# The weight sums of a blocked down projection: VectorE adds, or adding DMAs issued by GpSimd

## The chip, the cores and the metric

The kernel runs on one core of one Trainium2 chip. The core's engines, by the profile's names: PE (TensorE, matmuls; PEld is its loading of weights), DVE (VectorE, elementwise), ACT (ScalarE, elementwise with a function), POOL (GpSimd, elementwise and general) and SP (SyncE, which issues most DMAs). They run side by side, each through its own list of instructions in order, and wait for each other by semaphores. The metric is the device time of one execution in microseconds (us); less is better.

## The reference

The reference is a stack of two encoder layers on 512 tokens of width 1024, all in float32. Each layer mixes tokens (windowed and dilated attention, gates, an output projection, a layer norm) and then runs an MLP. What matters here is the MLP and the norm behind it:

```python
mlp = jnp.einsum('bsf,fd->bsd', jnp.square(jax.nn.relu(
    jnp.einsum('bsd,df->bsf', x, w_up[i]))), w_down[i])
...
x = _layer_norm(DEEPNORM_ALPHA * x + mlp + ple, ln2_g[i], ln2_b[i])
```

`w_up` is 1024 x 4096 and `w_down` 4096 x 1024 in each layer.

## The kernel before

**Precision.** Every float32 operand of a matmul is split in two: a high half (a cast to the type that TensorE takes, by ScalarE, line 225) and a low half (the operand less its high half, by VectorE, line 226). `split` does both. A product of matrices takes three matmuls (high by high, high by low, low by high). Weights come from HBM in chunks of 128 x 1024 numbers (512 KB) that SyncE loads (line 240, tiles `wst`), are split into `whi` and `wlo`, and are used two chunks later.

**Up projection.** The 4096 hidden columns go in four quarters (`q` from 0 to 3), each in eight tiles of 128 columns in the order `UP_ORDER`. Each tile takes 24 matmuls (lines 271 to 273). `Down.hidden` (lines 1013 to 1035) evacuates it: ScalarE takes the ReLU (line 1016), GpSimd squares it (line 1024), and ScalarE and VectorE make the high and low halves of the operands of the down projection: `a11`, `ax` and the sums `sm`. The last of them in a quarter (line 1035, `sml`) is kept as `ready`.

**Down projection.** Within a quarter, the product of the hidden part (as a 2 x 2 block matrix, tokens by hidden) with a 1024 x 1024 block of `w_down` (2 x 2 quadrants) is made in seven block products instead of eight, in the manner of Strassen and Winograd. The table `PRODUCTS` lists them: the operand from the hidden side, the operand from the weights' side, the accumulator, and whether it starts afresh. On the weights' side four of the seven operands are sums of quadrants. With the quadrants called b11, b12, b21 and b22 they are

- T1 = b11 + b12 (product 2), T2 = b11 + b12 + b22 (product 3), T4 = b11 + b12 + b22 + b21 (product 6), all three made one after the other in the tile that b11 was loaded into;
- T3 = b12 + b22 (product 5), made in the tile of b12.

Products 0, 1 and 4 use b11, b21 and b22 as they are. Each quadrant of 512 x 512 lies in two tiles of 128 x 1024 (`c` = 0 and 1), so that a quarter has eight raw tiles of 512 KB and eight sums; two layers of four quarters make 64 loads and 64 sums. `Down.load` (line 988) has SyncE load the eight tiles (line 993); `Down.cut` (line 1006) splits a raw tile as it stands into a set of high and low halves; `Down.add` (line 1002) makes the next sum in place. A sum in the tile of b11 may be made only after the cut before it has read the tile, and the next cut needs the sum: cut b11, add, cut T1, add, cut T2, add, cut T4. With `c` = 0 the halves go into `whi` and `wlo` (three of each, shared with the weights of the up projection), with `c` = 1 into `dhi` and `dlo` (four of each).

`Down.product` (line 1037) makes a block product in two halves of 12 matmuls (line 1051), first over the tiles with `c` = 0 and then with `c` = 1 for each half. Each half's accumulator is evacuated by VectorE (`gather`, line 1070; `spread`, line 1061) into the residual tiles `yt` and into `v`.

**Order.** TensorE runs in the order in which the code is written (`manual_schedule`). The other engines' instructions are put in order by the compiler, by dependences and by a simulation of its own; it makes the cuts and sums with `c` = 1 up to a quarter ahead, during the products of the quarter before. In two places the code sets order itself: `behind` puts the cuts and sums that follow a half product on VectorE behind `ready` (`tc.issue_after`, which queues the block's instructions behind the named one on the named one's engine), and behind the last quarter TensorE, VectorE and ScalarE all follow the code. During the seven products T2 with `c` = 0 is made between product 0's calls of `behind` and product 3: the cut of T1 and the sum of T2 are called behind the second half of product 0, the cut of T2 behind the second half of product 1.

GpSimd makes the squares in the up projection and has no work in the products. SyncE issues all loads in order; the next quarter's raw tiles are loaded as soon as the cuts and sums that read the buffers are done. The program sets the scratch for dynamic DMAs to 1024 bytes per partition.

Of the kernel before, what the change touches and what calls it, by code (L numbers as in the profile page):

```python
# [14 lines left out]
ALU = mybir.AluOpType  # L15
# [5 lines left out]
P = 128  # L21
# [179 lines left out]
def build(nc, tc, plan, down, xT, pT, wst, vec, sink, cst, outT):  # L201
# [3 lines left out]
    with ctx:  # L205
# [4 lines left out]
        def bank(tag, name):  # L210
            return pp.tile([P, 512], F32, tag=tag, name=name, bufs={"mm": 3, "s": 2, "pt": 2, "o": 1}[tag])
# [18 lines left out]
        down_at = {key: int(offs[len(plan) + n]) for n, (key, _) in enumerate(down)}  # L230
        ready, fetched = {}, {}
        at = [0, 0, 0]
# [18 lines left out]
        def ahead(last, further=0):  # L251
            while at[1] < len(plan) and at[1] <= max(last, further):
                fetch(at[1])
                at[1] += 1
                if at[1] - 1 <= last:
                    prep(at[2])
                    at[2] += 1
            while at[2] < len(plan) and at[2] <= last:
                prep(at[2])
                at[2] += 1  # L260

        def weights(key, look=LOOK, further=0):
            c = at[0]
            assert plan[c][0] == key, (plan[c][0], key)
            at[0] += 1
            ahead(c + look, c + further)
            return ready.pop(c)

        def mm3(ps, w, i, x, start, stop):
            s = slice(i * P, (i + 1) * P)  # L270
            nc.tensor.matmul(ps, w[0][:, s], x[0], start=start, stop=False)  # L271
            nc.tensor.matmul(ps, w[0][:, s], x[1], start=False, stop=False)  # L272
            nc.tensor.matmul(ps, w[1][:, s], x[0], start=False, stop=stop)  # L273

        def linear(key, xs, ps=None):
            w = weights(key)
            if ps is None:
                ps = bank("mm", "ps_" + "_".join(str(v) for v in key))
            for i, x in enumerate(xs):
                mm3(ps, w, i, x, i == 0, i == len(xs) - 1)  # L280
            return ps
# [527 lines left out]
        class Norm:  # L809
# [3 lines left out]
            def add(self, out, ps, y):  # L813
                if self.alpha == 1.0:
                    nc.vector.tensor_tensor(out, ps, y, ALU.add)
                else:
                    nc.vector.scalar_tensor_tensor(out, y, self.alpha, ps, ALU.mult, ALU.add)
# [79 lines left out]
            def behind(self, ins):  # L897
                tc.add_manual_dep(ins.ins, self.last.ins.name, mybir.DependencyInfo(
                    mybir.DependencyClass.Sync, mybir.DependencyReason.DATA), reason="statistics first")
# [59 lines left out]
        class Down:  # L959
# [28 lines left out]
            def load(self, q):  # L988
                for d, j in ((0, 0), (1, 0), (1, 1), (0, 1)):
                    for c in range(2):  # L990
                        r = self.qp.tile([P, 1024], F32, name=f"raw{self.l}_{q}_{j}{d}{c}", tag=f"raw{j}{d}{c}", bufs=1)
                        o = down_at[self.l, q, j, d, c]
                        nc.sync.dma_start(r, wst[o:o + P * 1024].rearrange("(p n) -> p n", p=P))
                        self.raw[j, d, c] = r

            def chain(self, n, c):

                b11, b12, b21, b22 = (self.raw[j, d, c] for j, d in ((0, 0), (0, 1), (1, 0), (1, 1)))
                return {"B11": (b11, None), "T1": (b11, b12), "T2": (b11, b22), "T4": (b11, b21),
                        "B22": (b22, None), "B21": (b21, None), "T3": (b12, b22)}[self.PRODUCTS[n][1]]  # L1000

            def add(self, n, c):
                to, other = self.chain(n, c)
                nc.vector.tensor_tensor(to, to, other, ALU.add)  # L1004

            def cut(self, q, n, c):
                pool, tag, bufs = (self.qp, "d", 4) if c else (wp, "w", 3)
# [137 lines left out]
        def pool(name, side="left"):  # L1145
            c = ExitStack()
            return c.enter_context(tc.tile_pool(name=name, bufs=1, side=side, reuse_waits="tile")), c.close
# [3 lines left out]
        for l in range(DEPTH):  # L1151
# [96 lines left out]
            dn = Down(l, qp, None)  # L1248

            def residual_turned(a):  # L1250
                for d in range(2):
                    tp = bank(("pt", "s")[a % 2], f"yT{l}_{a}_{d}")
                    for i in range(4):
                        nc.tensor.transpose(tp[:, i * P:(i + 1) * P], y[4 * d + i][:, a * P:(a + 1) * P], ident)
                    nc.scalar.copy(dn.y[a][:, d * 512:(d + 1) * 512], tp)
# [3 lines left out]
            with tc.manual_schedule(engines={PE}):  # L1259
                pss = []  # L1260
                for i in range(2):
                    pss.append(linear((l, ("up", 0, UP_ORDER[i])), X))
                    residual_turned(2 * i)
                    residual_turned(2 * i + 1)
                yp_close()
                p0_close()
                hp, hp_close = pool(f"hp{l}", "right")
                dn.hp = hp
                dn.operands()
                for q in range(FQ):  # L1270
                    for i, m in enumerate(UP_ORDER):
                        if not i:
                            dn.load(q)
                        if q or i > 1:
                            w = weights((l, ("up", q, m)), (2, 2, 2, 2, 2, 1, 1, 0)[i], min(3, 7 - i))
                            ps = bank("mm", f"ps_up{l}_{q}_{m}")
                            for k, x in enumerate(X):
                                mm3(ps, w, k, x, k == 0, k == KT - 1)
                        else:
                            ps = pss[i]  # L1280
                        dn.hidden(q, m, ps)
                        if i == 2:
                            dn.cut(q, 0, 1)
                        if q == FQ - 1 and i in (1, 2):
                            dn.spread(i - 1, dn.v[i - 1])
                        if i == 3:
                            dn.add(2, 1)
                            dn.cut(q, 1, 1)
                        if i == 4:
                            dn.add(5, 1)  # L1290
                        if i == 5:
                            dn.cut(q, 0, 0)
                        if i == 6:
                            dn.add(2, 0)
                            dn.add(5, 0)
                            dn.cut(q, 2, 1)
                        if i == 7:
                            dn.cut(q, 1, 0)
                            dn.add(3, 1)
                            dn.cut(q, 3, 1)  # L1300
                            dn.add(6, 1)
                    def behind(n, s):

                        with tc.issue_after(dn.ready.ins):
                            if n < 4:
                                if s:
                                    dn.cut(q, n + 2, 0)
                                    if n in (0, 1):
                                        dn.add((3, 6)[n], 0)
                                elif n:  # L1310
                                    dn.cut(q, n + 3, 1)
                            elif n == 4:
                                if not s:
                                    dn.cut(q, 6, 0)
                            elif s:
                                ahead(at[0] + n - 5, at[0] + 2)
                        if q == FQ - 1 and n == 1:
                            dn.moments(s, 0)

                    for n in range(7 if q < FQ - 1 else 4):  # L1320
                        dn.product(q, n, lambda s: behind(n, s))
                if not last:
                    ph, pl = (qp.tile([P, 2, S], F32R, name=f"p{e}{l + 1}", tag=f"raw11{i}", bufs=1) for i, e in enumerate("hl"))
                    pf = qp.tile([P, 2, S], F32, name=f"pf{l + 1}", tag="raw100", bufs=1)
                    nc.sync.dma_start(pf, pT[l + 1])
            q = FQ - 1
# [78 lines left out]
```

## Time and profile before

| | |
|---|---|
| median of 3 runs | 1571.31 us (1571.17 to 1573.22) |
| the profiled execution's own time | 1573.54 us |
| its span, first to last instruction | 1571.8 us |
| mean granted TensorE clock | 0.996 of full speed |
| DMA traffic | 143.37 MB, mean 91 GB/s |
| instructions of the sums (line 1004) | 64 on VectorE |
| loads of raw tiles (line 993) | 64 of 512 KB, median 4.4 us from issue to landing |

How to read the profile: a row of a group gives line, engine, operation, what it writes and reads (buffer numbers left out, so that all raw tiles are `raw`), the shape, the count, then busy us and the mean ns of one, then the engine's idle time ahead of it with what ended that ("releaser"). A row in order of time gives the start in us, the duration in us, engine, line, operation, tiles, and in brackets the idle time ahead and its releaser; neighbours of one kind are merged ("x2"). A row of a stretch gives its bounds, its length, and for PE, PEld, DVE, ACT and POOL the busy time with the number of instructions, then the granted clock, the share of the DMA engines and GB/s. A row of a line's answer gives the count, the shortest, median and longest duration in ns, and the first and last start. Rows of waits give us in total and how many times. Matmuls overlap: each shows as 0.39 us though one follows another in less. A DMA's "landing" is counted from its issue.

### The profile page before, as it was taken

How to read it: one execution, taken by the hardware profiler on the slowest of the kernel's cores; microseconds unless marked ns; L12 is line 12 of the kernel's file. 1: busy time of each engine (PE TensorE's matmuls, PEld its weight loads, DVE VectorE, ACT ScalarE, POOL GpSimd, SP SyncE). 2: the span in 40 equal slices, each digit the busy share in tenths (PEclk: the TensorE clock that was granted, in tenths of full speed). 3: DMA queues.
4: the chain of work that ended last, by engine and by line, in shares of the span. 5: the costliest groups of instructions: out<-in, count | busy, mean ns of one | idle time of the engine just before them, and what ended most of it. 6: DMA issues, size and time to landing. Idle time of an engine off the chain costs nothing.

```text
span 1571.8 us, 19688 instructions
## 1 busy us (share of the span) xinstructions
PE 1533.4 (98%) x7482; PEld 1254.0 (80%) x7482; DVE 1079.9 (69%) x1759; ACT 741.6 (47%) x1237; POOL 288.4 (18%) x208
## 2 busy tenths in 40 slices
PE   8999999999999999999899999999999999999997
PEld 6777888878888888888677778888887888888886
DVE  6878674454947777686868786744549476777867
ACT  4666554333644443434445665543336444434343
POOL 1010100157111111202000101101572111112020
PEclk9999999999999999999999999999999999999999
DMA  6212122232532414141132112223325324241401
GB/s 216 68 54 67 55 82 85 90 104 77 221 94 69 132 56 151 49 148 41 40 106 68 54 57 66 78 79 99 95 79 206 103 75 128 65 149 46 142 1 54
DMA packets 42736, 143.37 MB, mean 91 GB/s; under 512 B 5136, under 2 KB 7312, under 8 KB 42640
## 3 DMA queue, kind: packets, MB, share of 16 engines
q1 hardware_dynamic: 42064, 142.03, 28.4%
q8 instruction: 59, 0.97, 0.3%
q14 instruction: 37, 0.30, 0.1%
q10 hardware_dynamic: 576, 0.07, 0.0%
HBM read 139.98 MB, written 2.10 MB: 90 GB/s over the span
## 4 chain that ended last, share of the span: by engine, by line
PE 86%; DVE 8%; ACT 3%; issue 2%; DMA 1%; SPq 0%; ACTq 0%; DVEq 0%
PE dn L1051 16%; PE ps_up L273 7%; PE ps_up L272 7%; PE ps_up L271 7%; DVE wlo L226 2%; PE sa L399 1%; PE pta L377 1%; PE ps_start L271 1%; PE ps_start L272 1%; PE sb L399 1%; PE ps_start L273 1%; PE ya L271 1%; PE ya L273 1%; PE ya L272 1%; PE ps_pg L272 1%
## 5 line engine op out<-in xcount | busy, mean ns | idle before, releaser
L226 DVE TENSOR_TENSOR wlo<-wst,whi 128x1024 fp32r<-128x1024 f32 (+1 forms) x197 | 261.7, 1332 | 184.6 <-ACT whi L225 167.8
L225 ACT CAST whi<-wst 128x1024 fp32r<-128x1024 f32 (+1 forms) x197 | 202.3, 1029 | 352.8 <-PE ps_up L272 106.7
L1024 POOL TENSOR_TENSOR hr<-r 128x512 f32<-128x512 f32 x64 | 102.1, 1595 | 568.5 <-ACT r L1016 568.5
L271 PE MATMUL ps_up<-xhi,whi 128*128 128x512 f32 x480 | 186.9, 389 | 0.0
L273 PE MATMUL ps_up<-xhi,wlo 128*128 128x512 f32 x480 | 186.7, 389 | 0.0
L272 PE MATMUL ps_up<-xlo,whi 128*128 128x512 f32 x480 | 186.7, 389 | 0.0
L225 ACT CAST whi<-raw 128x1024 fp32r<-128x1024 f32 x56 | 58.0, 1052 | 101.4 <-PE ps_up L272 62.0
L272 PEld LDWEIGHTS ps_up<-xlo,whi 128*128 128x128 f32 x480 | 90.1, 188 | 18.8
L271 PEld LDWEIGHTS ps_up<-xhi,whi 128*128 128x128 f32 x480 | 90.1, 188 | 18.7
L273 PEld LDWEIGHTS ps_up<-xhi,wlo 128*128 128x128 f32 x480 | 90.1, 188 | 18.5
L225 ACT CAST dhi<-raw 128x1024 fp32r<-128x1024 f32 x56 | 58.8, 1052 | 82.8 <-PE dn L1051 59.5
L1070 DVE TENSOR_TENSOR yt<-yt,dn 128x512 f32<-128x512 f32 x96 | 65.3, 682 | 43.4 <-PE dn L1051 43.4
L1004 DVE TENSOR_TENSOR raw<-raw,raw 128x1024 f32<-128x1024 f32 x64 | 86.4, 1350 | 0.9 <-DMA raw<-wst 0.7
L226 DVE TENSOR_TENSOR wlo<-raw,whi 128x1024 fp32r<-128x1024 f32 x56 | 68.2, 1221 | 17.8 <-ACT whi L225 17.8
L226 DVE TENSOR_TENSOR dlo<-raw,dhi 128x1024 fp32r<-128x1024 f32 x56 | 68.2, 1220 | 5.1 <-ACT dhi L225 5.1
L336 POOL TENSOR_TENSOR sw_qb<-sw_qb,ct 128x512 f32<-128x512 f32 x12 | 18.4, 1536 | 181.9 <-DVE sw_qb L334 181.9
L1051 PE MATMUL dn<-whi,smh 128*128 128x512 f32 x128 | 50.1, 394 | 0.7 <-DVE yt L1070 0.7
L1051 PE MATMUL dn<-wlo,smh 128*128 128x512 f32 x128 | 50.6, 395 | 0.2
L1211 POOL TENSOR_TENSOR gate<-gate,gate 128x512 f32<-128x512 f32 x16 | 25.0, 1585 | 140.2 <-DVE gate L1210 140.2
L1051 PE MATMUL dn<-whi,sml 128*128 128x512 f32 x128 | 49.9, 390 | 0.0
L1051 PE MATMUL dn<-dhi,smh 128*128 128x512 f32 x128 | 49.9, 389 | 0.0
L1051 PE MATMUL dn<-dlo,smh 128*128 128x512 f32 x128 | 49.8, 389 | 0.0
(1015 smaller groups left out, 4048.0 us busy)
## 6 DMA issues: line engine op xcount, KB each, us to landing
wst<-wst SPq DMA_DIRECT2D x187, 512.0 KB, 3.6
raw<-wst SPq DMA_DIRECT2D x64, 512.0 KB, 4.4
wst<-wst SPq DMA_DIRECT2D x10, 256.0 KB, 2.7
xs<-xT SPq DMA_DIRECT2D x8, 256.0 KB, 4.7
outT<-nt SPq DMA_DIRECT2D x8, 256.0 KB, 2.2
ct<-cst SPq DMA_DIRECT2D x2, 960.0 KB, 8.0
pf<-pT SPq DMA_DIRECT2D x4, 256.0 KB, 4.0
pf<-pT SPq DMA_DIRECT2D x1, 512.0 KB, 3.5
```

Of the source, the lines that this page charges most:

```text
L225: nc.scalar.copy(hi, src)
L226: nc.vector.tensor_tensor(lo, src, hi.bitcast(F32), ALU.subtract)
L271: nc.tensor.matmul(ps, w[0][:, s], x[0], start=start, stop=False)
L272: nc.tensor.matmul(ps, w[0][:, s], x[1], start=False, stop=False)
L273: nc.tensor.matmul(ps, w[1][:, s], x[0], start=False, stop=stop)
L336: nc.gpsimd.tensor_tensor(sw, sw, cc["sin"], ALU.mult)
L399: nc.tensor.matmul(ss[r][:, col], q[a][rs, qs], k[b][rs, ks], start=n == 0, stop=n == 2)
L1004: nc.vector.tensor_tensor(to, to, other, ALU.add)
L1024: nc.gpsimd.tensor_tensor(h.rearrange("p s t -> p (s t)"), r, r, ALU.mult)
L1051: nc.tensor.matmul(ps[s], a[:, k, tok], w[b][:, cols], start=first and not (k or m), stop=k == 3 and m == 2, skip_group_check=True)
L1070: return nc.vector.tensor_tensor(to, to, ps, ALU.subtract if n in (2, 4, 5) else ALU.add)
L1211: nc.gpsimd.tensor_tensor(g, g, ga[t], ALU.add)
```

## The change

The sums are no longer VectorE instructions with both quadrants in SBUF. GpSimd issues a DMA that reads the other quadrant from HBM again and adds it to the tile in place. The calls of `add` get the quarter as an argument and stand where they stood; `at` is the slice of the packed weights from which `load` takes a quadrant too. The call inside `behind` (the sums of T2 and T4 with `c` = 0) is still inside `tc.issue_after(dn.ready.ins)`, which names a VectorE instruction.

```diff
-                        o = down_at[self.l, q, j, d, c]
-                        nc.sync.dma_start(r, wst[o:o + P * 1024].rearrange("(p n) -> p n", p=P))
+                        nc.sync.dma_start(r, self.at(q, j, d, c))
                         self.raw[j, d, c] = r
 
+            def at(self, q, j, d, c):
+                o = down_at[self.l, q, j, d, c]
+                return wst[o:o + P * 1024].rearrange("(p n) -> p n", p=P)
+
             def chain(self, n, c):
 
                 b11, b12, b21, b22 = (self.raw[j, d, c] for j, d in ((0, 0), (0, 1), (1, 0), (1, 1)))
-                return {"B11": (b11, None), "T1": (b11, b12), "T2": (b11, b22), "T4": (b11, b21),
-                        "B22": (b22, None), "B21": (b21, None), "T3": (b12, b22)}[self.PRODUCTS[n][1]]
-
-            def add(self, n, c):
+                return {"B11": (b11, None), "T1": (b11, (0, 1)), "T2": (b11, (1, 1)), "T4": (b11, (1, 0)),
+                        "B22": (b22, None), "B21": (b21, None), "T3": (b12, (1, 1))}[self.PRODUCTS[n][1]]
+
+            def add(self, q, n, c):
                 to, other = self.chain(n, c)
-                nc.vector.tensor_tensor(to, to, other, ALU.add)
+                nc.gpsimd.dma_start(to, self.at(q, *other, c), accum_op=ALU.add)
...
                         if i == 3:
-                            dn.add(2, 1)
+                            dn.add(q, 2, 1)
                             dn.cut(q, 1, 1)
                         if i == 4:
-                            dn.add(5, 1)
+                            dn.add(q, 5, 1)
...
                         if i == 6:
-                            dn.add(2, 0)
-                            dn.add(5, 0)
+                            dn.add(q, 2, 0)
+                            dn.add(q, 5, 0)
                             dn.cut(q, 2, 1)
                         if i == 7:
                             dn.cut(q, 1, 0)
-                            dn.add(3, 1)
+                            dn.add(q, 3, 1)
                             dn.cut(q, 3, 1)
-                            dn.add(6, 1)
+                            dn.add(q, 6, 1)
...
                                     if n in (0, 1):
-                                        dn.add((3, 6)[n], 0)
+                                        dn.add(q, (3, 6)[n], 0)
```

## The prediction

> **What bounds the kernel now.** I read the page first (busy times, the chain that ended last, the costliest groups, the DMA issues), then the answers for the lines that the diff touches, then one down projection in order of time.
>
> ```profile
> span 1571.8 us, 19688 instructions
> ...
> PE 1533.4 (98%) x7482; PEld 1254.0 (80%) x7482; DVE 1079.9 (69%) x1759; ACT 741.6 (47%) x1237; POOL 288.4 (18%) x208
> ...
> PE 86%; DVE 8%; ACT 3%; issue 2%; DMA 1%; SPq 0%; ACTq 0%; DVEq 0%
> ...
> L225 ACT CAST whi<-raw 128x1024 fp32r<-128x1024 f32 x56 | 58.0, 1052 | 101.4 <-PE ps_up L272 62.0
> ...
> L1004 DVE TENSOR_TENSOR raw<-raw,raw 128x1024 f32<-128x1024 f32 x64 | 86.4, 1350 | 0.9 <-DMA raw<-wst 0.7
> ```
>
> TensorE is busy 98% of the span and carries 86% of the chain. The 64 adds that the change removes take 86.4 us of VectorE, an engine with 31% idle. So time can only come from gaps of TensorE, and those of the stage that holds the adds are small. One answer gives busy times over the stretches of the two MLP stages (up and down projections and the norm behind them), the next is the tail of the answer for the product's line, the third is TensorE's waits in the first of the two stretches:
>
> ```profile
> 440.00:782.00 342.00, 337.56 (x1498) 276.77 (x1498) 243.19 (x300) 147.19 (x187) 51.06 (x32) 1.00 0.28 87
> 1220.00:1571.80 351.80, 342.81 (x1527) 281.68 (x1525) 247.27 (x317) 149.45 (x193) 51.03 (x32) 0.99 0.26 83
> ...
>   DVE yt L1070: 4.2, 12
>   DVE wlo L226: 2.7, 6
>   ACT whi L225: 2.6, 6
> ...
> PE dn L1051 <- DVE yt L1070: 1.0, 3, 0.5
> ```
>
> TensorE (the second figure) is idle 4.4 of 342.0 us and 9.0 of 351.8 us. The products waited 4.2 us for their accumulators' evacuation and 2.7 us for low halves of weights, counted over matmuls and weight loads together; 4.2 + 2.7 = 6.9 us is all that a freer VectorE could ever return.
>
> **The change part by part.** Removed: 64 VectorE instructions (1220 ns each alone). Added: 64 DMAs of 512 KB from HBM, each issued by GpSimd. Where VectorE had two operands in SBUF, the second now comes from HBM, so the second quadrant's own load matters no more for the sum; the first operand must have landed and its last split (a ScalarE cast for the high half, a VectorE subtraction for the low half) must have read it before the DMA may start, and the next split must wait until the DMA has landed. So each sum turns from one VectorE instruction into an issue, a transfer and a semaphore. What counts is where a sum stands tightly between two splits. Here is the second quarter of layer 0, products 2 and 3, VectorE, then ScalarE, TensorE, SyncE and GpSimd:
>
> ```profile
> 577.34 1.23 DVE L1035 TENSOR_TENSOR sml<-sr,smh 128x1024 fp32r<-128x1024 f32 x1 [1.34 <-ACT smh L1034]
> 578.48 1.22 DVE L226 TENSOR_TENSOR wlo<-raw,whi 128x1024 fp32r<-128x1024 f32 x1
> 579.62 0.68 DVE L1070 TENSOR_TENSOR yt<-yt,dn 128x512 f32<-128x512 f32 x1
> 580.21 1.22 DVE L226 TENSOR_TENSOR dlo<-raw,dhi 128x1024 fp32r<-128x1024 f32 x1
> 581.35 1.22 DVE L1004 TENSOR_TENSOR raw<-raw,raw 128x1024 f32<-128x1024 f32 x1
> ...
> 585.23 1.22 DVE L226 TENSOR_TENSOR wlo<-raw,whi 128x1024 fp32r<-128x1024 f32 x1
> ...
> 582.60 2.00 ACT L225 CAST whi<-raw 128x1024 fp32r<-128x1024 f32 x2 [0.81 <-DVE raw L1004]
> ...
> 585.84 0.39 PE L1051 MATMUL dn<-dhi,sml 128*128 128x512 f32 x1
> 586.07 0.39 PE L1051 MATMUL dn<-whi,smh 128*128 128x512 f32 x1
> 586.50 0.50 PE L1051 MATMUL dn<-wlo,smh 128*128 128x512 f32 x1
> ...
> 581.50 4.16 SPq L993 DMA_DIRECT2D raw<-wst  x2
> ...
> 615.44 1.53 POOL L1024 TENSOR_TENSOR hr<-r 128x512 f32<-128x512 f32 x1 [43.14 <-ACT r L1016]
> ```
>
> The subtraction at 578.48 is the low half of T1 (first half, c = 0); it may not go earlier, since the code queues it behind the `sml` at 577.34. It ends at 579.70. The add at 581.35 makes T2 in the same tile; the first cast at 582.60 is T2's high half, the subtraction at 585.23 its low half, and product 3 uses them at 586.07 and 586.50. Matmuls follow at 0.23 us (585.84 to 586.07), so the second one wanted 586.30 and is 0.20 us late already. There is no slack behind the low half; the slack lies between 579.70 and 582.60 (the add waits for two other VectorE instructions) and between the cast's end at 583.65 and 585.23.
>
> With the DMA the path is: issue at 579.70, landing L later, cast 1.05, subtraction 1.22, and three handovers of about 0.05 (586.45, where the subtraction ends, to 586.50): the matmul comes at 579.70 + L + 1.05 + 1.22 + 0.15 = 582.12 + L. Today it comes at 586.50. So each such place costs L - 4.4 us of TensorE once L is over 4.4. GpSimd is idle there: its next work is at 615.44 after 43.14 us, so the waiting DMA blocks nothing on its queue. This place comes once in each quarter of each layer, 8 times; the answer for the adds' line says the same of today:
>
> ```profile
>   ACT whi L225: 6.5, 8
> ...
> L993 SPq DMA_DIRECT2D raw<-wst x64: 327/328/620, 398.1 to 1463.2; - x64
> ...
> DMA to landing us min/median/max: 3.5/4.4/10.8
> ...
> wst<-wst SPq DMA_DIRECT2D x187, 512.0 KB, 3.6
> raw<-wst SPq DMA_DIRECT2D x64, 512.0 KB, 4.4
> wst<-wst SPq DMA_DIRECT2D x10, 256.0 KB, 2.7
> ...
> L1024 POOL TENSOR_TENSOR hr<-r x64: 1042/1592/1875, 446.9 to 1520.1; 128x512 f32<-128x512 f32 x64
> ```
>
> ScalarE waited for the add 8 times, 6.5 us, or 0.81 each: the row at 582.60.
>
> **L** is shown by no row, since no DMA here adds and none is issued by GpSimd. From both sides: a plain load of the same 512 KB lands at best after 3.5 us, typically 3.6 alone, and a crowded one after 10.8. Estimate between: 256 KB take 2.7 and 512 KB 3.6, so 512 KB move in about 1.8 and 1.8 are fixed. An adding DMA also reads its destination: nothing if that runs under the first read, another 1.8 if both reads pass through the same engines in turn; I take 1.8, since the same DMA engines carry both. A load shares them: the raw load that SyncE issues at 581.50 falls into every such transfer, and loads with neighbours take 4.4 instead of 3.5, so 0.9. GpSimd's issue: between SyncE's 0.33 us and the 1.6 of a GpSimd instruction, so 0 to 1.3 more; I take 0.3, since an issue moves no data. L = 3.6 + 1.8 + 0.9 + 0.3 = 6.6, range 3.5 to 10.8. Sum: 8 x (6.6 - 4.4) = 17.6 us.
>
> [...]
>
> The other sums, with the rows of the same quarter and the next (the first two: T1 with c = 0 and its cast; then T1 with c = 1, its cast, T2's cast, the next weights' split), and of the stretch before the first quarter:
>
> ```profile
> 556.68 2.06 DVE L1004 TENSOR_TENSOR raw<-raw,raw 128x1024 f32<-128x1024 f32 x1
> ...
> 569.64 1.05 ACT L225 CAST whi<-raw 128x1024 fp32r<-128x1024 f32 x1 [2.50 <-PE ps_up L272]
> ...
> 598.55 1.22 DVE L1004 TENSOR_TENSOR raw<-raw,raw 128x1024 f32<-128x1024 f32 x1
> ...
> 602.92 1.05 ACT L225 CAST dhi<-raw 128x1024 fp32r<-128x1024 f32 x1 [0.26 <-PE dn L1051]
> ...
> 608.51 1.06 ACT L225 CAST dhi<-raw 128x1024 fp32r<-128x1024 f32 x1 [0.26 <-PE dn L1051]
> 613.77 1.05 ACT L225 CAST whi<-wst 128x1024 fp32r<-128x1024 f32 x1 [4.20 <-PE ps_up L272]
> ...
> 413.56 2.00 ACT L225 CAST dhi<-raw 128x1024 fp32r<-128x1024 f32 x2
> 416.23 1.37 ACT L1239 ACTIVATE tg<-ps_pg,vhalf 128x512 f32<-128x512 f32 x2 [0.67 <-PE ps_pg L273]
> ...
> 407.19 1.21 DVE L226 TENSOR_TENSOR dlo<-raw,dhi 128x1024 fp32r<-128x1024 f32 x1
> ```
>
> T1 with c = 0: from 556.68 to its cast at 569.64 are 13 us, which cover any L up to there; T3 has as much. T4 with c = 0 may start when T2's low half is done (586.45) and is wanted by product 6, three products of 24 matmuls at 0.23 us behind 586.07, at 602.4; less both splits that leaves 13 us. With c = 1 the sums are made a quarter ahead: T1 issues at 598.5 or a little before and lands at 605 (cast today at 602.92), T2 lands 6.6 and two splits later, at 614 (cast today at 608.51). ScalarE, in order, is held until then, and behind it waits the next weights' split of 613.77. Weights are split two tiles ahead (11 us), so this is free up to L of about 10; without that cover it costs 2 L - 11 a quarter.
>
> Before the first quarter of a layer the lead is thinner: T1's sum may start at 408.4 and would land at 415.0 or later; its cast, the second of 413.56, is at 414.5, and the evacuation at 416.23 queues behind. Between 0 (the compiler orders ScalarE otherwise) and 6 us (T1 and T2 each hold it for about 3); I take 1 for each of the two layers, 2 us. GpSimd's squares queue behind a waiting issue in the up projection for a microsecond or so; VectorE, free of an add beside them, has room for that: 0, and 1 us a quarter if not. SyncE's loads for the next quarter start no later, as the tiles of `b21` come free earlier.
>
> Returned: the waits of TensorE for evacuation in this stage (1.0 us in the row above, of the kind that the freed VectorE ends): -1. Sum: 17.6 + 2 - 1 = 18.6, about 19 us. The profiled execution took 1573.5 us with its span of 1571.8; it becomes about 1592.5. The median of the three runs is 1571.31, 2.2 below the profiled one, so 1590.
>
> **The rivals.** A change under 0.2%, 3.1 us, can't be told from none.
>
> Hidden: L is at most 4.4 to 4.8, as a plain load is (3.5 to 4.4). Then the DMA fits where the add and its queue were, 8 x (0 to 0.4) less 1: 1570 to 1573. For it: plain loads reach it. Against: it needs the second read, the neighbour and GpSimd's issue to cost nearly nothing together. [...] Chance 0.16.
>
> Faster: L is under 4.4 and the freed VectorE ends the waits for it. The 0.20 us at 8 places are 1.6, evacuation at most 4.2, together 5.8 and 1565; half of it, since waits of loads and matmuls are counted side by side, 1568. It decides when the low half at 585.23 can start as soon as the cast is done, 1.5 us earlier than today, which needs L under 4.2. Chance 0.09.
>
> Much slower: adding runs at a fraction of the plain rate, or ScalarE and VectorE, held in order by late sums with c = 1, hold TensorE too. From L = 9 on: 8 x 4.6 = 37, with 6 before each first quarter some 49, and at 10.8 some 63: 1608 to 1634. Chance 0.17.
>
> Not as said: were the sums' DMAs made to wait for each other or for SyncE's loads, L would hold that wait too; they come one by one, so it is no case of its own.
>
> **How the numbers follow.** My forecast (L from 4.8 to 9, 1574 to 1608) has 0.58, its likeliest point 1590. Slower 0.58 + 0.17 = 0.75, same 0.16, faster 0.09. The range 1570 to 1614 leaves out the faster case (0.09) and most of the much slower one (0.11).
>
> **What would show it.** Right: TensorE gets a gap of about 2 us before product 3 in all 8 quarters, put down to ScalarE's cast and behind it to the DMA; the median landing of GpSimd's DMAs is near 6.6; VectorE's busy time falls by about 86 us; matmul times are unchanged. Wrong: landings near 4 and no gap (hidden), gaps in the up projection or before the first quarter (order, not L), or gaps behind GpSimd's squares.

## The result, and the profile after

The median after is 1590.01 us (four runs, 1589.0 to 1592.31), against 1571.74 for the kernel before (four runs, 1571.17 to 1573.22): a ratio of 1.0113, 95% interval 1.01 to 1.0125 (the intervals below are of the same kind), so 18.3 us slower. The profiled execution took 1592.31 us, 18.8 more than the profiled one of before.

These are lines of the profile page of the changed kernel: span, busy time by engine, the chain that ended last, the casts of the c = 1 tiles, and the DMAs into `raw`: SyncE's plain loads, then GpSimd's adding ones. Everything behind the diff has moved down by three lines (the add was line 1004 and is 1007, the products' matmuls were 1051 and are 1054).

```profile
span 1590.3 us, 19844 instructions
...
PE 1540.6 (97%) x7482; PEld 1257.3 (79%) x7482; DVE 1004.7 (63%) x1695; ACT 738.2 (46%) x1237; POOL 331.7 (21%) x272
...
PE 81%; DVE 8%; DMA 5%; ACT 3%; issue 2%; POOL 0%; SPq 0%; ACTq 0%; POOLq 0%; DVEq 0%
...
L225 ACT CAST dhi<-raw 128x1024 fp32r<-128x1024 f32 x56 | 58.8, 1051 | 180.3 <-DMA raw<-wst 125.1
...
raw<-wst SPq DMA_DIRECT2D x64, 512.0 KB, 5.7
raw<-wst POOLq DMA_DIRECT2D x64, 512.0 KB, 5.6
```

VectorE has lost 75.2 us of work, and the chain shows what replaced it: DMA went from 1% to 5% of the span. ScalarE's casts of the c = 1 tiles now wait 125.1 us for `raw` to land; before, they waited mostly for TensorE. (`raw<-wst` stands for a plain load as well as for a sum's DMA: which of the two ended a wait has to be looked up.) An adding DMA lands 5.6 us after its issue (median), and SyncE's own loads of `raw` now take 5.7 instead of 4.4.

To see where the time went, count the matmuls that fit into a fixed stretch. The next two answers, of before and then of after, give busy time and count (TensorE first) for two stretches of the MLP stages of the two layers that both kernels fill:

```profile
440.00:772.00 332.00, 330.87 (x1468) 271.82 (x1468) 236.86 (x290) 138.43 (x174) 51.06 (x32) 1.00 0.28 86
...
1222.00:1560.00 338.00, 337.09 (x1502) 276.83 (x1500) 241.51 (x302) 142.41 (x180) 51.03 (x32) 1.00 0.25 80
```

```profile
440.00:772.00 332.00, 325.74 (x1439) 266.57 (x1438) 200.57 (x247) 136.98 (x173) 68.39 (x59) 1.00 0.51 133
...
1222.00:1560.00 338.00, 330.16 (x1453) 270.18 (x1452) 200.67 (x246) 140.93 (x179) 69.87 (x61) 0.99 0.51 129
```

29 and 49 matmuls fewer, at 0.227 us each (three in 0.68), are 6.6 and 11.1 us: 17.7 of the 18.8 us went inside these stages. (The idle time grew by 12.1 us only, since the record of a matmul behind a gap is longer: 0.5 instead of 0.39 us.) What TensorE waited for between 440 and 1565 us, first before, then after (us, times, longest):

```profile
PE dn L1051 <- DVE yt L1070: 1.4, 4, 0.5
```

```profile
PE dn L1054 <- ACT whi L225: 5.0, 10, 1.0
PE dn L1054 <- DVE wlo L226: 4.6, 6, 0.8
...
PE dn L1054 <- DVE yt L1073: 2.4, 3, 1.2
...
PE ps_up L273 <- DVE wlo L226: 2.0, 2, 1.7
```

The first two rows, 16 waits, are two for each of the 8 quarters: product 3 waits for the high and then for the low half of T2 (in the last quarter of each layer both waits are for high halves). The other two rows, five waits, belong to the turn from one quarter to the next. First the tight place of the prediction, second quarter of layer 0, by engine:

```profile
580.72 1.22 DVE L226 TENSOR_TENSOR wlo<-raw,whi 128x1024 fp32r<-128x1024 f32 x1
...
588.92 1.23 DVE L226 TENSOR_TENSOR wlo<-raw,whi 128x1024 fp32r<-128x1024 f32 x1 [1.38 <-ACT whi L225]
...
587.84 2.94 ACT L225 CAST whi<-raw 128x1024 fp32r<-128x1024 f32 x3 [3.80 <-DMA raw<-wst]
...
582.36 0.88 POOL L1007 DMA_DIRECT2D raw<-wst  x1 [7.82 <-DVE wlo L226]
...
588.01 0.39 PE L1054 MATMUL dn<-dhi,sml 128*128 128x512 f32 x1
588.94 0.49 PE L1054 MATMUL dn<-whi,smh 128*128 128x512 f32 x1 [0.54 <-ACT whi L225]
590.20 0.50 PE L1054 MATMUL dn<-wlo,smh 128*128 128x512 f32 x1 [0.77 <-DVE wlo L226]
590.54 0.39 PE L1054 MATMUL dn<-whi,sml 128*128 128x512 f32 x1
```

T1's low half ends at 581.94, GpSimd's DMA starts 0.42 us later, and T2's cast starts at 587.84. Product 3 then starts 0.93 us behind the matmul before it and goes on after another 1.26 us, where 0.23 is the pace: 0.70 + 1.03 = 1.73 us lost, against 0.20 before, so 1.5 a place and 12 us in eight.

The turn to the next quarter: GpSimd issues the sums of T3 (c = 0) and of the next quarter's T1 (c = 1) together (one row, x2). ScalarE, VectorE and TensorE there:

```profile
604.25 1.77 POOL L1007 DMA_DIRECT2D raw<-wst  x2 [11.04 <-DVE dlo L226]
...
613.84 1.05 ACT L225 CAST dhi<-raw 128x1024 fp32r<-128x1024 f32 x1 [7.46 <-DMA raw<-wst]
...
614.91 1.23 DVE L226 TENSOR_TENSOR dlo<-raw,dhi 128x1024 fp32r<-128x1024 f32 x1 [6.46 <-ACT dhi L225]
616.06 1.28 DVE L1073 TENSOR_TENSOR yt<-yt,dn 128x512 f32<-128x512 f32 x2
617.25 2.35 DVE L226 TENSOR_TENSOR wlo<-wst,whi 128x1024 fp32r<-128x1024 f32 x2
...
618.53 0.50 PE L273 MATMUL ps_up<-xhi,wlo 128*128 128x512 f32 x1 [0.23 <-DVE wlo L226]
```

T1's cast comes 9.6 us after the first of the two issues. VectorE stands idle for 6.46 us, because the low half of T1 is its next instruction; two evacuations and the up projection's next weights queue behind. Here it costs TensorE 0.4 us, and the same wait costs 1.7 us at 1329.54: these are the two waits of the last of the four rows.

The three waits for evacuations (692.22, 1316.20 and 1488.24) go back to something else. There VectorE's next instruction is the low half of the next quarter's b11 (c = 1), and that tile comes by SyncE's plain load. The load lands 6.3 to 7.3 us after its issue, with adding DMAs in flight beside it; the same load took 3.5 to 4.7 us before.

### The profile page after: what moved, and what is told of

It reads as the page before. It is cut to its first block, busy times and chain, and to the rows that moved or that the text cites. A ratio compares the mean times of both kernels' runs of the same rounds, so it can differ in the third digit from the quotient of the medians.

```text
span 1590.3 us, 19844 instructions
## 1 busy us (share of the span) xinstructions
PE 1540.6 (97%) x7482; PEld 1257.3 (79%) x7482; DVE 1004.7 (63%) x1695; ACT 738.2 (46%) x1237; POOL 331.7 (21%) x272
## 4 chain that ended last, share of the span: by engine, by line
PE 81%; DVE 8%; DMA 5%; ACT 3%; issue 2%; POOL 0%; SPq 0%; ACTq 0%; POOLq 0%; DVEq 0%
PE dn L1054 11%; PE ps_up L273 7%; PE ps_up L272 7%; PE ps_up L271 7%; DMA raw<-wst 5%; DVE wlo L226 3%; PE sa L399 1%; PE sb L399 1%; PE pta L377 1%; PE ps_start L272 1%; ACT whi L225 1%; PE ps_start L271 1%; PE ps_start L273 1%; PE ya L273 1%; PE ya L272 1%
## 5 line engine op out<-in xcount | busy, mean ns | idle before, releaser
L225 ACT CAST dhi<-raw 128x1024 fp32r<-128x1024 f32 x56 | 58.8, 1051 | 180.3 <-DMA raw<-wst 125.1
L1007 POOL DMA_DIRECT2D raw<-wst x64 | 56.1, 890 | 404.4 <-DVE dlo L226 137.6
L1027 POOL TENSOR_TENSOR hr<-r 128x512 f32<-128x512 f32 x64 | 93.4, 1471 | 169.6 <-ACT r L1019 169.6
L1054 PE MATMUL dn<-dhi,sml 128*128 128x512 f32 x128 | 50.3, 393 | 0.0
```

Of the source, the lines that this page charges most:

```text
L225: nc.scalar.copy(hi, src)
L1007: nc.gpsimd.dma_start(to, self.at(q, *other, c), accum_op=ALU.add)
L1027: nc.gpsimd.tensor_tensor(h.rearrange("p s t -> p (s t)"), r, r, ALU.mult)
L1054: nc.tensor.matmul(ps[s], a[:, k, tok], w[b][:, cols], start=first and not (k or m), stop=k == 3 and m == 2, skip_group_check=True)
```

## Experiments

All comparisons are with runs of the kernel before on the same chip: median 1573.22 us, and 1572.39 for three of them (the plain load by SyncE, and of the early split the kernels with c = 1 alone and with all but T1). The selective kernels keep the changed kernel's text and choose per sum, by product number `n` and half `c` (product 3 is T2, 2 is T1, 5 is T3, 6 is T4):

```diff
-                nc.gpsimd.dma_start(to, self.at(q, *other, c), accum_op=ALU.add)
+                if CONDITION:
+                    nc.gpsimd.dma_start(to, self.at(q, *other, c), accum_op=ALU.add)
+                else:
+                    nc.vector.tensor_tensor(to, to, self.raw[(*other, c)], ALU.add)
```

The theory was the prediction's: the loss is the place of T2 with c = 0. Its rival: the loss is traffic and order, spread over all 64 sums.

**T2 with c = 0 alone back on VectorE** (`CONDITION` is `(n, c) != (3, 0)`).

> As changed, but T2 with c = 0 (8 of the 64 sums) is again a VectorE add; the other 56 stay adding DMAs. Theory (the place): the gap before product 3 was 8 x 1.5 = 12 us of the 18, so the time falls to about 1577 (1575 to 1580), and the rest is what late sums with c = 1 do to ScalarE and VectorE. Rival (traffic): the loss goes with the number of adding DMAs, through the DMA engines and GpSimd, 18 / 64 = 0.29 us each, so only 2.3 us come back: 1588. Rival (first quarter): most is lost where the lead is thin, before the first quarter of a layer: 1588 or above.

1582.62 us (1580.75 to 1582.85), ratio 1.0058, interval 1.0043 to 1.0073: 9.4 slower than before, so about half of the loss is gone and half stays. Both theories missed. What is left, in TensorE's waits over the same stretch:

```profile
PE dn L1057 <- DVE yt L1076: 4.9, 8, 1.3
PE ps_up L273 <- DVE wlo L226: 2.1, 1, 2.1
```

The waits for T2's halves have vanished, those for evacuations have grown from 2.4 to 4.9 us. There are two costs.

**T2 with c = 0 alone by DMA** (`(n, c) == (3, 0)`).

> As before, but T2 with c = 0 alone (8 sums) is an adding DMA issued by GpSimd. The place: 8 x 1.5 = 12 us, 1583 to 1584, with the gap before product 3 as in the changed kernel. Traffic: 8 x 0.29 = 2.3 us, 1574.

1583.27 us (1582.44 to 1584.04), 1.0065 (1.005 to 1.008): 10.0 slower from 8 DMAs of 64. TensorE's waits, and the answer for the DMAs' line (us from issue to landing):

```profile
PE dn L1057 <- DVE wlo L226: 4.5, 6, 0.8
PE dn L1057 <- ACT whi L225: 4.1, 10, 0.6
PE dn L1057 <- DVE yt L1076: 0.7, 2, 0.4
```

```profile
DMA to landing us min/median/max: 5.2/5.4/5.6
```

The place is shown: eight sums that stand between two splits cost as much as the theory says, with no other sum moved. The waits for evacuation fell from 1.4 to 0.7 us.

**The 32 sums with c = 1 alone by DMA** (`c`).

> As before, but the 32 sums with c = 1, which are made a quarter ahead, are adding DMAs; all with c = 0 are VectorE adds. The place: late sums hold ScalarE and VectorE in order and cost the 5 us or so that T2 does not explain: 1575 to 1578, seen as waits of TensorE for evacuations and weights at the turn from one quarter to the next. Traffic: 32 x 0.29 = 9 us, 1581.

1578.57 us (1578.0 to 1582.35), 1.0039 (1.0026 to 1.0053): 5.4 slower, in the evacuations:

```profile
PE dn L1057 <- DVE yt L1076: 6.2, 8, 1.4
```

Eight waits instead of four, 6.2 us instead of 1.4. The longest, on ScalarE, VectorE and TensorE:

```profile
682.31 1.05 ACT L225 CAST dhi<-raw 128x1024 fp32r<-128x1024 f32 x1 [6.98 <-DMA raw<-wst]
...
683.39 1.23 DVE L226 TENSOR_TENSOR dlo<-raw,dhi 128x1024 fp32r<-128x1024 f32 x1 [2.65 <-ACT dhi L225]
...
687.87 0.47 PE L1057 MATMUL dn<-whi,axh 128*128 128x512 f32 x1 [1.43 <-DVE yt L1076]
```

VectorE reaches the evacuation late, since the low half of 683.39 is ahead of it. But the cast of 682.31 does not wait for a sum. It waits for a plain load, the next quarter's b11 (c = 1), which SyncE issued at 674.73, 1.54 us behind an adding DMA. The landing of this load, and of the same load before (issued at 673.34):

```profile
DMA to landing us min/median/max: 7.5/7.5/7.5
```

```profile
DMA to landing us min/median/max: 4.7/4.7/4.7
```

All six waits at the turns (the other two are inside the last quarters, 0.36 us each) go back to this load, 6.4 to 7.5 us from issue to landing, where before it took 3.5 to 4.7. T1's own sum lands 5.0 to 5.5 us after its issue here, and no wait of TensorE goes back to it. So the waits behind these 5.4 us go back to a plain load that lands late beside an adding DMA, and not to a sum that lands late.

**T1, T3 and T4 with c = 0 alone by DMA** (`not c and n != 3`).

> As before, but T1, T3 and T4 with c = 0 (24 sums, the ones with 13 us of cover) are adding DMAs; T2 and all with c = 1 are VectorE adds. The place: no loss, 1570 to 1572. Traffic: 24 x 0.29 = 7 us, 1579.

1573.89 us (1572.31 to 1576.54), 1.0008 (0.9998 to 1.0017): no loss from 24 DMAs, since each has some 13 us of cover by the prediction's count. The added traffic of these 24 costs nothing that can be measured; issued 4.3 to 5.4 us ahead of the load of b11 (c = 1), they leave it at 3.9 to 4.5 us. The three groups add to 10.0 + 5.4 + 0.7 = 16.1 us, all together cost 18.3; their intervals are too wide to call that a difference.

**What does T2 wait for in the transfer?** Two kernels put T2 with c = 0 on a plain load, whose sum is thus left out: one issued by GpSimd, one by SyncE. Against the kernel with that sum alone by DMA:

```diff
-                    nc.gpsimd.dma_start(to, self.at(q, *other, c), accum_op=ALU.add)
+                    nc.gpsimd.dma_start(to, self.at(q, *other, c))
```

> As before, but in place of T2's sum with c = 0 GpSimd issues a DMA that does not add: it puts the quadrant there alone, so that the addition is left out of these 8 sums. Against the same with adding (10 us over the kernel before, 5.4 us to landing) it prices the adding. If the second read costs what the prediction took, 1.8 us, it lands 3.6 us after its issue and the gap is nearly gone: 0 to 2 us over. If adding costs nothing and GpSimd's path does: still 5.4 us and 10 over.

1573.41 us (1572.49 to 1574.81), 1.0006 (0.9997 to 1.0015).

```profile
DMA to landing us min/median/max: 3.8/3.9/4.1
```

The second kernel has `nc.sync.dma_start` in that line:

> As before, but in place of T2's sum with c = 0 SyncE issues a plain load of the quadrant, so that the addition is left out of these 8 sums. Against the same issued by GpSimd (3.9 us from issue to landing, 0.2 us over the kernel before) it prices GpSimd's path. The prediction took 0.3 us; a landing 3.5 us after its issue, some 0.4 less, and a time within 1 us of the kernel before either way.

1573.08 us (1570.33 to 1575.57), 0.9999 (0.999 to 1.0009).

```profile
DMA to landing us min/median/max: 3.4/3.5/3.6
```

So in this place, with the same bytes, a load by SyncE takes 3.5 us, GpSimd's issue adds 0.4 and the adding 1.5: 5.4. Without the adding the whole loss of 10 us is gone.

**The changed kernel with T1's split queued earlier.** T1's low half (c = 0) is held in VectorE's queue behind `sml`, by `issue_after`. This kernel calls its split at the end of the up projection, so that T2's sum can start sooner; all 64 sums are by DMA.

```diff
                             dn.add(q, 6, 1)
+                            dn.cut(q, 2, 0)
...
                                 if s:
-                                    dn.cut(q, n + 2, 0)
+                                    if n:
+                                        dn.cut(q, n + 2, 0)
```

> As changed (all 64 sums by adding DMAs), but the split of T1 with c = 0 is called at the end of the up projection and not behind `ready`, so that T2's DMA may start some 8 us earlier. The place: T2 lands before the code wants it, the 8 gaps of 1.7 us before product 3 go, and what is left is what T2 on VectorE left, or 1.6 us less: 7 to 9 us over the kernel before, about 1581. Traffic, or a slow adding DMA as such: the transfers are as many and as long, so nothing comes back: 18 over.

1582.43 us (1578.1 to 1584.11), 1.0057 (1.004 to 1.0073): 9.2 slower. No wait of product 3 for T2's halves is left, with as many transfers: the length of the chain of dependent steps was the cause there. What is left is the turn of the quarter, worse than before the edit. TensorE's waits, then GpSimd, ScalarE, VectorE and TensorE at one turn:

```profile
PE dn L1054 <- DVE yt L1073: 7.3, 3, 2.7
PE ps_up L273 <- DVE wlo L226: 4.7, 2, 2.9
```

```profile
600.41 1.77 POOL L1007 DMA_DIRECT2D raw<-wst  x2 [9.30 <-DVE yt L1073]
...
611.35 1.05 ACT L225 CAST dhi<-raw 128x1024 fp32r<-128x1024 f32 x1 [9.72 <-DMA raw<-wst]
...
612.43 1.23 DVE L226 TENSOR_TENSOR dlo<-raw,dhi 128x1024 fp32r<-128x1024 f32 x1 [8.72 <-ACT dhi L225]
...
616.04 0.50 PE L273 MATMUL ps_up<-xhi,wlo 128*128 128x512 f32 x1 [2.86 <-DVE wlo L226]
```

T1's cast (c = 1) comes 10.9 us after the first issue. The next theory: the sums of T3 (c = 0) and T1 (c = 1) are issued together and share the DMA engines, and T1's low half then holds VectorE. That fits the two waits for weights (4.7 us). The three for evacuations (7.3 us) go back to the load of b11 again, which lands 8.2 to 8.7 us after its issue there.

**The earlier split with all sums on VectorE** (`False`) **and with the c = 0 sums by DMA** (`not c`).

> As before (all sums on VectorE), with the same earlier split of T1. Today product 3 waits 0.2 us in 6 of 8 quarters; the place gives at most 8 x 0.2 = 1.6 us: 0 to 1.6 us under the kernel before. If the earlier split delays `ready` on VectorE instead, the same or some us slower.

> All 32 sums with c = 0 by adding DMAs, all with c = 1 on VectorE, with the earlier split of T1. The place: every DMA has its cover, so no loss, and up to 1.6 us gained: 1571.5 to 1573.5 where the kernel before takes 1573. Traffic: 32 x 0.29 = 9 us over.

All on VectorE: 1567.73 us (1567.15 to 1569.12), 0.9968 (0.9955 to 0.998), 5.5 faster than before. The 32 with c = 0 by DMA: 1567.70 us (1566.29 to 1569.09), 0.9968 (0.9955 to 0.998), the same 5.5. Both beat both kernels, and by more than was expected of them. Moving half of the sums to DMAs costs nothing once T2 has its lead; the gain belongs to the split. With all sums on VectorE, ScalarE at T2, and the stretch from 440 to 772 us:

```profile
579.09 2.00 ACT L225 CAST whi<-raw 128x1024 fp32r<-128x1024 f32 x2 [2.43 <-DVE raw L1010]
```

```profile
440.00:772.00 332.00, 331.82 (x1483) 274.47 (x1481) 237.21 (x290) 140.77 (x178) 53.23 (x32) 1.00 0.27 86
```

T2's cast is 3.5 us earlier than before (582.60) and TensorE waits not once for a product's weights or evacuation between 440 and 1565 us. In 332 us 15 matmuls more run than before, 3.4 us in one layer. The expectation had counted only the 0.20 us before one matmul of product 3 (1.6 us in all). With the waits for evacuations, 1.4 us before, that makes 3.0; where the other 2.5 us come from stays open.

**The earlier split with the c = 1 sums alone by DMA** (`c`).

> Earlier split of T1 with c = 0; the 32 sums with c = 1 by adding DMAs, all with c = 0 on VectorE. In the kernel with the earlier split and all sums by DMA, T1 with c = 1 was issued 0.6 us behind T3 with c = 0 and landed after 10 us, which held VectorE and through it weights and evacuations. Theory (two DMAs in a row): alone it lands after 5.4 us, and the time is that of the early split on VectorE (5.5 us under the kernel before) plus the 5 us that sums with c = 1 cost by themselves: about 1573, 0 to 2 us from the kernel before. Rival (any sum with c = 1 by DMA holds VectorE as long): 9 us over, as with all sums by DMA.

1567.86 us (1566.61 to 1570.89), 0.9971 (0.9959 to 0.9983): 4.5 faster than before, which its interval doesn't tell from the 5.5 with all on VectorE, and better than either side expected. At the turn (GpSimd, ScalarE, VectorE):

```profile
597.97 0.87 POOL L1008 DMA_DIRECT2D raw<-wst  x1 [5.93 <-DVE dlo L226]
...
604.88 1.05 ACT L225 CAST dhi<-raw 128x1024 fp32r<-128x1024 f32 x1 [2.88 <-DMA raw<-wst]
...
605.96 1.23 DVE L226 TENSOR_TENSOR dlo<-raw,dhi 128x1024 fp32r<-128x1024 f32 x1 [1.87 <-ACT dhi L225]
```

Issued alone, T1's sum lets its cast start after 6.9 us instead of 10.9, VectorE is held 1.87 us instead of 8.72, and TensorE doesn't notice. The load of b11 (c = 1) is issued ahead of the adding DMA in four of six quarters here, and 0.3 to 0.5 us behind it in the other two (1.5 to 2.8 us behind with the old split); it lands after 4.4 to 5.2 us, and its low half holds VectorE for at most 1.3 us. Neither half of the sums costs anything that can be measured alone; both together cost 1582.43 - 1567.73 = 14.7 us.

**The earlier split with all by DMA but T1 with c = 1** (`(n, c) != (2, 1)`).

> Earlier split of T1 with c = 0; all sums by adding DMAs but T1 with c = 1 (8 sums), which is a VectorE add. Theory (the low half of T1 with c = 1 holds VectorE): without that wait the gaps at the turn of the quarters go, and it is 4 to 5.5 us under the kernel before: 1568 to 1570. Rival: T2 with c = 1, late as well, takes its place: 3 us over or more, 1576 and up.

1567.63 us (1566.58 to 1567.84), 0.9963 (0.9951 to 0.9976): 4.8 faster than before by the medians, with 56 of 64 sums by DMA. Taking one sum a quarter off the DMAs ends the loss. It does not single out the hold that the theory names: the other sums are issued at other times here too, no adding DMA is in flight beside the load of b11 (c = 1), and that load is back at 3.6 to 4.5 us, so both holds end at once. A late landing is now that of T2 with c = 1, at the same turn, on ScalarE:

```profile
611.37 1.05 ACT L225 CAST dhi<-raw 128x1024 fp32r<-128x1024 f32 x1 [4.56 <-DMA raw<-wst]
```

By then the weights and evacuations that TensorE needs are done, and no wait for them is listed.

## Why the prediction was right, and where not

**The place and the mechanism** of its main term hold: product 3, in all 8 quarters, ScalarE's cast behind the DMA. Its formula, the matmul at T1's end plus L plus two splits, gives L = 590.20 - 581.94 - 2.42 = 5.8 us; it had taken 6.6. 8 x (5.8 - 4.4) is 11.2 where it had 17.6.

**The terms of L.** Measured: 3.5 for the plain load (it took 3.6), 0.4 for GpSimd (0.3), 1.5 for adding (1.8), and 0.4 from the split's end to the start of the issue, which it had not counted. Its 0.9 for a neighbouring load did not appear: the eight DMAs of T2 alone land in 5.2 to 5.6 us, in the last quarter, where no load of a next quarter runs, as in the others. That term is the mis-sized one. If 1.8 of the plain transfer move bytes, as the prediction estimated from the landings of 256 and 512 KB, adding makes 3.3 of them, 1.8 times. The packets come near that: the queue of GpSimd's eight DMAs moved 4.19 MB in both kernels and took 1.6% of the 16 DMA engines' time with the adding, 0.8% without. That a second read through the same engines is what takes this time fits both figures; no run shows it by itself.

**The rival "Hidden"** falls on the adding alone: GpSimd's plain load at 3.9 us made no loss, as that rival's condition (at most 4.4 to 4.8) said, and the adding one is at 5.4.

**The turn of the quarter was put at nothing, and that failed.** For the c = 1 sums the prediction said "free up to L of about 10", and for the next quarter's loads that they "start no later". Alone these sums cost 5.4 us, at landings of 6.0 us in the median. The loads start no later, but land later: the prediction priced a transfer beside another on the sum's DMA, 0.9 us, where it did not appear, and not on the plain load, which landed later beside the sum's DMA (6.4 to 7.5 us instead of 3.5 to 4.7). Behind the load stands VectorE's low half of b11, and behind that, in order, the evacuations, which have no lead of two tiles. A hold by "late sums" it named in its much slower rival. That hold is real where two sums are issued together, and costs 2.0 us (two waits for weights) in the changed kernel, at 9.6 and 10.7 us from the first issue to T1's cast.

**Before the first quarter** it took 2 us; nothing shows there. The DMAs are slow among the loads, as it feared, and ScalarE is held; but TensorE is dense. ScalarE, and TensorE's stretch, in the changed kernel:

```profile
420.52 1.05 ACT L225 CAST dhi<-raw 128x1024 fp32r<-128x1024 f32 x1 [5.61 <-DMA raw<-wst]
```

```profile
395.00:441.00 46.00, 46.00 (x205) 38.09 (x204) 34.09 (x40) 26.72 (x37) 11.21 (x9) 1.00 0.77 236
```

**Returned.** It took 1 us back. T2 alone costs 11.2 by the formula and 10.0 measured, which agrees, but the interval of the 10.0 (8 to 13 us) can't settle 1 us. VectorE's busy time fell by 75.2 us, not 86, and GpSimd's waiting issues held up nothing that TensorE saw.

**The sum.** 17.6 + 2 - 1 met 18.3 because errors cancel: the tight place is about 6 us cheaper, nothing is lost before the first quarter where 2 us were booked, and the other sums, booked at nothing there, cost 8 to 9 us together (18.3 - 10.0, and the 9.4 with T2 back on VectorE). The forecast was right in its sign and place, and right in its size partly by luck.

**Open.** The waits at the turn are traced to the load of b11 and to the second of two sums, but no run changes one of them alone. That an adding DMA in flight slows the load is read from its times: 3.4 to 4.7 us in the kernels where none is in flight beside it, 5.8 to 7.5 where one went out 1.5 to 4.0 us ahead, with the old split. With the early split the spacing alone does not settle it: issues within 0.5 us of each other gave 4.4 and 4.7 us with the c = 1 sums alone, and 4.9, 8.2, 8.3 and 8.7 with all by DMA. That is also why it stays open how the c = 1 sums come to cost at most 1 us there. That two sums issued together delay each other through the DMA engines is argued in the same way (9.6 and 10.9 us to T1's cast, against 6.9 alone), and no run shows it by itself.

## What to carry to other kernels

An operation moved to a DMA is priced by its time from release to landing at the tightest place, not by the engine time that it frees: 24 sums with cover cost nothing here, 8 without cost 10 us. Then look at the transfers beside the new ones: a plain load that lands 3 us later holds the instruction that waits for it, and on its engine everything behind in order. Here that and one pair of sums made the turn nearly as dear as the tight place. And before moving work off an engine with idle time, look at what holds it in the queue: the order of one split was worth 5.5 us with no DMA at all.

## What the runs showed of the hardware that was not expected

One short gap of TensorE cost a second time. In the changed kernel the second quarter of layer 1 has its gap before product 3 as the others do, somewhat longer (idle 1.04 and 0.76 us, against 0.54 and 0.77 in the quarter shown above), and it falls into one stretch of 3.41 us; the granted clock (the column behind the engines' figures) is 0.5 in the stretch after it:

```profile
1383.95:1387.36 3.41, 1.77 (x6) 1.23 (x7) 2.54 (x3) 3.41 (x4) 0.86 (x1) 1.00 0.53 165
1387.36:1390.78 3.42, 3.42 (x9) 2.65 (x8) 1.01 (x2) 0.27 (x1) 0.87 (x1) 0.50 0.85 128
1390.78:1394.19 3.41, 3.41 (x16) 2.82 (x15) 2.14 (x4) 1.05 (x1) 0.00 (x0) 1.00 1.00 237
```

Nine matmuls instead of sixteen: about 1.6 us more for one gap of the eight. It happened once in the MLP stages of this profile. The kernel with T2 alone back on VectorE shows such a stretch at 1324.85 us, and the one with the early split and all by DMA at 617.41: a granted clock of 0.5 for 3.41 us, behind a stretch of 3.42 and 3.41 us in which TensorE was busy for 1.34 and 1.36 us. Here it was busy for 1.77 us of the 3.41 before. Why the clock fell behind this gap and not behind the other seven is not shown.

Two adding DMAs of 512 KB, issued back to back by GpSimd at a turn, let the cast that needs the second start 8.0 to 10.9 us after the first issue (changed kernel, and the one with the early split), where T2's alone lands in 5.4. A plain load of 512 KB by SyncE, issued 1.5 to 2.8 us behind an adding DMA, landed after 6.4 to 7.5 us, against 3.5 to 4.7 for the same load before. Before the first quarter, among SyncE's loads, the longest adding DMA took 14.5 us.
